# Attention and state-space heads in pairs: half-array products of two heads side by side

## The chip, the cores and the metric

One NeuronCore of one Trainium2 chip runs the whole network. The metric is the device time of one execution in microseconds (us); the time of a kernel is the median of its runs.

## The reference

The input is one sequence of 256 tokens with 1024 features, in float32. A first stack has a multi-head latent attention layer (MLA, 16 heads) with a dense SwiGLU, then a Mamba-2 layer (32 heads of 64 channels) with a mixture of eight experts. A second stack of two layers follows; each is a SwiGLU, a mixer and another SwiGLU. The mixer is what most of the change is about:

```python
h = _rms(x, mix_norm[l])
# native sparse attention (NSA), 8 heads of 64, 2 key/value groups: three softmaxes per head
o_a = gate_cmp * o_cmp + gate_sel * o_sel + gate_win * o_win
# block attention (MoBA), 8 heads of 64: with 256 tokens it is one causal softmax per head
y_a, y_b = o_a @ w_branch_nsa[l], o_b @ w_branch_moba[l]
x = x + (sigmoid(gate_a) * y_a + sigmoid(gate_b) * y_b) @ w_out[l]
```

At 256 tokens the window branch and the selected branch are both plain causal attention over all tokens, and the compressed branch has 15 keys (a block of 32 tokens every 16).

## The kernel before

Activations lie feature-major, [128 features, 256 tokens] per tile. A large product (`gemm`, `mm3`, lines 180 to 182) splits its weights into two float32r parts on ScalarE (`whi`, L153) and VectorE (`wlo`, L156) and makes three passes over 256 columns; a tile row of 256 weight columns is six such matmuls. Products of attention are plain float32, each in two passes, so a product shows as two records (x2) in the trace.

The tiles of PSUM come from four tags: `acc` (2 banks), `s` (3 banks, scores and some products), `sm` (2 banks, transposes and small things) and `po` (1 bank, outputs of attention, four heads in one bank). A tag's buffers are given out in the order of the program. The order of instructions on each engine is set when the kernel is built: a scheduler takes what its own timeline says is ready, earlier lines of the program first, and each engine then runs its list in that order. `keep_in_program_order` puts an instruction behind the one traced before it on its engine; other instructions can still come between.

In the mixer (`mixer`, twice) the order of the program is: compressed keys and values, keys and values of NSA, gates of the branches, `heads` (queries, keys) with the small products of `compress` mixed in, then eight heads of MoBA one by one, eight heads of NSA one by one (`nsa_head`), then the products for the two mixer gates (L1543, eight `gemm`s of 48 matmuls) and the branch and output products. The gate products need nothing of the attention, so the scheduler puts them into its gaps.

A MoBA head has its scores for the first and the second tile of queries (L1514, L1515; 64 rows of the array, since a head has 64 features), two mask products in bfloat16 with the identity (L1516, L1517), `softmax` (L864 to L877: two maxima on VectorE, two exponentials with sums on ScalarE, two scalings on VectorE, three transposes on TensorE, one copy on ScalarE) and two products with the values (L1520, L1521; 64 columns of the array). Even heads use rows or columns 0 to 63, odd heads 64 to 127.

An NSA head does both tiles of queries and all three branches at once: L1573 (second tile of queries against 512 keys of both branches) and L1575 (first tile), masks L1574, L1576, L1579, compressed scores L1577 and L1578 (15 columns each), maxima L1582 to L1584, six exponentials L1590, six scalings L1596, eight transposes L1602 and L1603, and for each branch the products L1613, L1614 and L1615 (the compressed one with 15 rows of the array). Its scores take two `s` banks.

MLA's heads (L839 to L846) have 128-row scores; only their products with the values are half the array. Mamba's heads have the products L1017 and L1018 with 64 columns, from `heads` inside `mamba`.

Of the kernel before, what the change touches and what calls it, by code (L numbers as in the profile page):

```python
# [17 lines left out]
P = 128  # L18
# [14 lines left out]
def _consts():  # L33
# [11 lines left out]
    # rope of the first block: rows 64..127 hold cos (32 rows) and -sin, +sin (16 rows each)  # L45
# [19 lines left out]
    # rope of the second block, feature-major, halves of 32 rows  # L65
# [8 lines left out]
    put("half2", np.stack([r < 64, r >= 64]))  # L74
    return np.concatenate(cols, 1)
# [5 lines left out]
class K:  # L81
    def __init__(self, tc, ins, out, ctx):
        self.tc, self.nc, self.i, self.out = tc, tc.nc, ins, out
        pool = lambda name, bufs, **k: ctx.enter_context(tc.tile_pool(name=name, bufs=bufs, **k))
        self.pc = pool("const", 1)
        self.pw = pool("w", 1)
        self.pn = pool("norm", 1)
        self.ps = pool("psum", 1, space=bass.MemoryType.PSUM)
        self.nraw, self.nhi, self.nlo, self.nslot = 5, 5, 4, 14
        self.fill = []  # L90
        self.fins = []
        self.lag = 0
# [5 lines left out]
        self.uid = 0  # L98

# [5 lines left out]
    # a tag's slots are given out in the order of the program: one tag for each role  # L105
# [26 lines left out]
    def parts(self, n, shape=None):  # L132
        """a pair of float32r tiles of n <= 1024 columns"""
# [9 lines left out]
    def split(self, src, pool=False):  # L143
        """[128, k, n...] float32 -> lists over k of high and low parts"""
# [16 lines left out]
    def load(self, w, k0, nk, n0, n, raw=None):  # L161
        """rows k0*128.. of w (K, N), columns n0..n0+n -> [128, nk, n]"""
# [5 lines left out]
    def wtiles(self, w, kt, n0, n, first=(), pool=False):  # L168
        """generator of (k, hi, lo): the row tiles of columns n0..n0+n, [128, n] each"""
# [7 lines left out]
    def mm3(self, out, whi, wlo, xhi, xlo, first, last):  # L177
        """out += w^T x in three float32r passes; w stationary"""
# [5 lines left out]
    def gemm(self, w, kt, n0, n, x, s=False):  # L184
        """feature-major: [n <= 256 features as 2 tiles, 256 tokens] in one bank; x = (hi, lo) [128, kt, 256]"""
# [5 lines left out]
    def gemm_steps(self, w, kt, n0, n, x, a, pool=False):  # L191
        """the same, a row tile of w at a time"""
# [8 lines left out]
    def rstd(self, *groups, bcast=True, fold=0, gap=0):  # L201
        """for each group (xs, d): [128, 256] in PSUM, (mean of squares + eps)^-1/2 of each token, on every partition"""
# [5 lines left out]
    def stats(self, *groups, fold=0):  # L208
        """halves of the means of squares + eps, token-major"""
# [21 lines left out]
    def fold(self, sqs, n):  # L231
        """adds up pairs of tiles before their products: none, those of the first pair, or all"""
# [8 lines left out]
    def sums(self, ms, sqs, first):  # L241
        """ms [128, 2]: sums over the features, token-major"""
# [7 lines left out]
    def square(self, x, part=None, new="sq"):  # L250
        """squares; added to part if there is one"""
# [7 lines left out]
    def rstd_tail(self, s, bcast=True):  # L259
        """s[:, 0]: halves of the means of squares + eps, token-major; broadcast of their ^-1/2"""  # L260
# [17 lines left out]
    def spread(self, r):  # L278
        """a token's r [128, 2] on every partition: [128, 256] in PSUM"""
# [7 lines left out]
    def norm(self, xs, d, g, hi, lo, shift=None, src=None, gap=0):  # L287
        """hi + lo = x * rstd * g (+ shift); g, shift: per-feature columns [128, len(xs)]"""
# [26 lines left out]
    def slot(self, pool, dt=F32, tag="g4", bufs=None):  # L315
        """a 4 KB tile [128, 4, 256]"""
# [10 lines left out]
    def setup(self, p):  # L327
# [12 lines left out]
        # warm the tensor engine while the first loads are under way  # L340
# [3 lines left out]
        # silu(c) as columns  # L344
# [4 lines left out]
        # the mean of the squares of each token  # L349
# [21 lines left out]
    def setup2(self):  # L371
# [17 lines left out]
        # skip weights as columns: head 2j on rows 0..63, head 2j + 1 on rows 64..127  # L389
# [8 lines left out]
    def rows(self, entries, tag, dma=None, t=None):  # L398
        """small vectors as rows of 128, transposed to columns"""
# [35 lines left out]
    def cond_mm(self, pr, rs, k0):  # L435
        """products of silu(c) with row tiles k0.., each in its own 32 columns of the array: they run at once"""
# [5 lines left out]
    def cond_sum(self, pr):  # L442
        """the sums of what cond_mm made, as columns"""
# [8 lines left out]
    def ada_steps(self, l, j, share=(), act=()):  # L452
        """closures: eight loads with their products, then the sum over partitions"""
# [40 lines left out]
    def fillers(self, jobs):  # L494
        """the steps of several jobs in a row; their sums are left to calls of fin()"""
# [51 lines left out]
        # the second mean of squares is r^2 times that of x first  # L547
# [35 lines left out]
    def resid(self, a, n0, g, last=True):  # L583
        """x += a g, for two tiles; last: what x gets last before its norm"""
# [51 lines left out]
    def rope1(self, tq, tk, p):  # L636
        """tables from the positions: rows 64.. cos, -sin, +sin; rows ..63 one"""
# [12 lines left out]
        # two pi in parts of eight bits, so that the products with n are exact  # L650
# [10 lines left out]
        # back into [-pi, pi]  # L661
# [11 lines left out]
    def mla(self):  # L673
        nc, i = self.nc, self.i
        v, mm = nc.vector, nc.tensor.matmul
        self.nslot, self.wpe = 4, 384
        with ExitStack() as c:
# [12 lines left out]
            # c_q 384 | c_kv 256 | rope 32 | rope with its halves exchanged 32  # L690
# [4 lines left out]
            def block(b):  # L695
                """the products with the two feature tiles of block b"""
# [92 lines left out]
            def latent(hl, g, xs):  # L789
                """the norm of the latents is applied to what is made of them"""  # L790
# [24 lines left out]
            # attention  # L815
            scale = float(np.float32(96.0 ** -0.5))
            um = p.tile([1, 192], BF16, name="um")
            v.memset(um[:, :64], 1.0)
            v.memset(um[:, 64:P], 0.0)
            v.memset(um[:, P:], NEG)  # L820
# [4 lines left out]
            for g in range(4):  # L825
# [7 lines left out]
                for hh in range(4):  # L833
                    if (g, hh) == (3, 0):
                        self.fin()
                    self.filler()
                    hd = g * 4 + hh
                    s = self.s([P, 384])
                    mm(s[:, :P], qT[:, hh, :P], kTa[:, hd, :P], start=True, stop=False, **kw)  # L839
                    mm(s[:, P:], qT[:, hh, P:], kTa[:, hd], start=False, stop=False, **kw)  # L840
# [3 lines left out]
                    o = po[(hh % 2) * 64 : (hh % 2) * 64 + 64, hh // 2]  # L844
                    mm(o, vs[:, 0, hd], pt[:, :T], start=True, stop=False, **kw)
                    mm(o[:, P:], vs[:, 1, hd], pt[:, T:], start=False, stop=True, **kw)  # L846
# [9 lines left out]
    def softmax(self, p, s, segs, scale, mult=None):  # L856
        """softmax of the column ranges `segs` of the scores s, transposed in blocks of 128"""
# [3 lines left out]
        w = s.shape[1]  # L861
        st = p.tile([P, 3, n], F32, tag="st", bufs=4, name=self.name("st"))
# [13 lines left out]
        pt = p.tile([P, 512], F32, tag="pt", bufs=4, name=self.name("pt"))[:, :w]  # L876
        nc.scalar.copy(pt, ptp)  # L877
        return pt

# [1 line left out]
    def mamba(self):  # L881
# [4 lines left out]
        with ExitStack() as c:  # L886
# [6 lines left out]
            def conv(n0, out):  # L893
                """out [128, 2, 256]: silu of the causal convolution of channels n0.. of xBC"""
# [13 lines left out]
            # dt: token-major, softplus; a = -exp(a_log)  # L908
# [18 lines left out]
            # log(1 + u) = 2 atanh(u / (2 + u))  # L927
# [11 lines left out]
            # running sums of dt a within each tile of tokens: columns and rows  # L939
# [50 lines left out]
            def tokens(g):  # L990
                """x dt, token-major"""
# [703 lines left out]
```

## Time and profile before

| what | value |
|---|---|
| time, median of 3 runs | 2753.67 us (2751.53 to 2759.7) |
| span of the profiled execution | 2753.1 us |
| TensorE (PE) busy | 2643.2 us, 96% |
| VectorE (DVE) busy | 2081.9 us, 76% |
| ScalarE (ACT) busy | 1578.1 us, 57% |
| GpSimd (POOL) busy | 521.4 us, 19% |
| mean granted TensorE clock | 0.970 of full speed |

Engines work at the same time, so the shares don't add up. Matmuls overlap in TensorE's pipeline: what a matmul costs is the distance from its start to the start of the next, which a timeline shows, not its own duration.

### The profile page before, as it was taken

The page shows a single profiled execution, that of the slowest core. Times are in us where ns is not written, and L with a number is a line of the kernel's source. Part 1 is how long each engine was busy: PE and PEld are TensorE (multiplying, and loading weights), DVE is VectorE, ACT ScalarE, POOL GpSimd, SP SyncE. Part 2 cuts the span into 40 slices and gives each one's busy share as a digit, 9 for nine tenths or more (in the row PEclk, how much of TensorE's full clock was granted, in tenths as well). Part 3 has the DMA queues.
Part 4 walks back from the last instruction along what each step waited for, and adds up shares of the span by engine and source line. Part 5 has one row for each costly group of instructions (what it writes and reads, how often), then busy time and mean ns, then how long its engine had stood idle before and what let it go on. Part 6 is the DMA issues. An engine that isn't in the chain of part 4 may idle for free.

```text
span 2753.1 us, 52105 instructions
## 1 busy us (share of the span) xinstructions
PE 2643.2 (96%) x21231; PEld 2531.5 (92%) x21231; DVE 2081.9 (76%) x2837; ACT 1578.1 (57%) x2330; POOL 521.4 (19%) x257
## 2 busy tenths in 40 slices
PE   7879987998999999999999999999999999999998
PEld 5779986987899999999999999978999999979998
DVE  5878999866999999899989756655755656666654
ACT  4534433663777877677777444655544444665543
POOL 4367894713100000000000110000110110000110
PEclk8979997999999999999999999999999999999999
DMA  8647775624999999899998556514555556415552
GB/s 298 216 145 239 243 230 170 216 84 132 306 350 326 369 357 352 281 355 328 365 348 290 173 180 217 157 39 146 184 181 188 184 177 212 154 36 166 182 180 94
DMA packets 577831, 608.99 MB, mean 221 GB/s; under 512 B 21563, under 2 KB 562768, under 8 KB 577584
## 3 DMA queue, kind: packets, MB, share of 16 engines
q1 hardware_dynamic: 577222, 605.26, 66.9%
q8 instruction: 168, 2.75, 0.4%
q0 software_dynamic: 176, 0.26, 0.1%
q14 instruction: 79, 0.65, 0.1%
q10 hardware_dynamic: 186, 0.07, 0.0%
HBM read 604.50 MB, written 1.05 MB: 220 GB/s over the span
## 4 chain that ended last, share of the span: by engine, by line
PE 59%; DVE 0%; POOL 0%; issue 0%; DVEq 0%; ACT 0%; POOLq 0%
PE acc L180 9%; PE acc L181 9%; PE acc L182 9%; PE s L181 3%; PE s L182 3%; PE s L180 3%; PE acc L1243 3%; PE acc L1241 3%; PE acc L1242 3%; PE acc L1264 1%; PE acc L1263 1%; PE acc L1265 1%; PE po L1613 1%; PE s L1573 1%; PE sm L1602 0%; PE sm L1414 0%
## 5 line engine op out<-in xcount | busy, mean ns | idle before, releaser
L156 DVE TENSOR_TENSOR wlo<-raw,whi 128x1024 fp32r<-128x1024 f32 (+1 forms) x815 | 1075.8, 1330 | 285.9 <-PE acc L182 190.6
L153 ACT CAST whi<-raw 128x1024 fp32r<-128x1024 f32 (+1 forms) x825 | 842.7, 1029 | 675.4 <-PE acc L181 384.2
L180 PE MATMUL acc<-hl,whi 128*128 128x256 f32 x2336 | 669.7, 287 | 1.1 <-ACT hl L304 1.1
L181 PE MATMUL acc<-hl,whi 128*128 128x256 f32 x2336 | 664.9, 285 | 5.0 <-DVE hl L305 5.0
L182 PE MATMUL acc<-hl,wlo 128*128 128x256 f32 x2336 | 664.8, 285 | 3.1 <-DVE wlo L156 3.0
L181 PEld LDWEIGHTS acc<-hl,whi 128*128 128x128 f32 x2336 | 444.9, 191 | 6.9 <-DVE hl L305 5.9
L182 PEld LDWEIGHTS acc<-hl,wlo 128*128 128x128 f32 x2336 | 444.9, 190 | 4.9 <-DVE wlo L156 4.1
L180 PEld LDWEIGHTS acc<-hl,whi 128*128 128x128 f32 x2336 | 445.3, 191 | 3.0 <-ACT hl L304 1.4
L1242 PE MATMUL acc<-wlo,xh 128*128 128x256 f32 x1408 | 397.6, 283 | 0.0
L1243 PE MATMUL acc<-whi,xl 128*128 128x256 f32 x1408 | 394.8, 281 | 0.4 <-DVE gr L1197 0.4
L1241 PE MATMUL acc<-whi,xh 128*128 128x256 f32 x1408 | 395.0, 281 | 0.0
L156 DVE TENSOR_TENSOR wlo<-more,whi 128x1024 fp32r<-128x1024 f32 x240 | 281.0, 1188 | 19.0 <-PE acc L1242 6.4
L153 ACT CAST whi<-more 128x1024 fp32r<-128x1024 f32 x244 | 246.2, 1022 | 51.1 <-PE acc L1243 23.7
L1243 PEld LDWEIGHTS acc<-whi,xl 128*128 128x128 f32 x1408 | 264.5, 188 | 0.7 <-DVE xl L1227 0.7
L1242 PEld LDWEIGHTS acc<-wlo,xh 128*128 128x128 f32 x1408 | 264.2, 188 | 0.2 <-DVE wlo L156 0.2
L1241 PEld LDWEIGHTS acc<-whi,xh 128*128 128x128 f32 x1408 | 264.1, 188 | 0.0
L182 PE MATMUL s<-hl,wlo 128*128 128x256 f32 x880 | 249.1, 283 | 0.4 <-DVE wlo L156 0.4
L181 PE MATMUL s<-hl,whi 128*128 128x256 f32 x880 | 249.4, 283 | 0.0
L180 PE MATMUL s<-hl,whi 128*128 128x256 f32 x880 | 249.1, 283 | 0.0
L256 POOL TENSOR_TENSOR part<-part,sq 128x512 f32<-128x512 f32 x20 | 31.1, 1553 | 1103.8 <-ACT sq L253 1103.8
L1264 PE MATMUL acc<-wlo,fh 128*128 128x256 f32 x704 | 195.9, 279 | 0.2 <-DVE wlo L156 0.2
L1265 PE MATMUL acc<-whi,fl 128*128 128x256 f32 x704 | 195.8, 279 | 0.0
(514 smaller groups left out, 5165.6 us busy)
## 6 DMA issues: line engine op xcount, KB each, us to landing
raw<-in_moe_w_gate_dram SPq DMA_DIRECT2D x49, 1024.0 KB, 6.5
raw<-in_moe_w_up_dram SPq DMA_DIRECT2D x49, 1024.0 KB, 7.7
raw<-in_ffn_wg_dram SPq DMA_DIRECT2D x44, 1024.0 KB, 5.2
raw<-in_ffn_wu_dram SPq DMA_DIRECT2D x44, 1024.0 KB, 5.2
more<-in_moe_w_gate_dram SPq DMA_DIRECT2D x39, 1024.0 KB, 8.1
more<-in_moe_w_up_dram SPq DMA_DIRECT2D x39, 1024.0 KB, 7.9
raw<-in_w_in_dram SPq DMA_DIRECT2D x38, 1024.0 KB, 5.0
fr<-in_ada_w_dram SPq DMA_DIRECT2D x72, 512.0 KB, 4.1
```

The source lines that it names most:

```text
L153: i = nc.scalar.copy(hi, src[:, k0 : k0 + m])
L156: (nc.gpsimd if pool else nc.vector).tensor_sub(lo, src[:, k0 : k0 + m], hi)
L180: mm(out, whi, xhi, start=first, stop=False, skip_group_check=True)
L181: mm(out, whi, xlo, start=False, stop=False, skip_group_check=True)
L182: mm(out, wlo, xhi, start=False, stop=last, skip_group_check=True)
L256: self.nc.gpsimd.tensor_add(part, part, o)
L1241: mm(a[:, b], xh[:, k], hi, start=b == 0 and k == 0, stop=False, skip_group_check=True)
L1242: mm(a[:, b], xh[:, k], lo, start=False, stop=False, skip_group_check=True)
L1243: mm(a[:, b], xl[:, k], hi, start=False, stop=k == 7, skip_group_check=True)
L1263: mm(a, fh[k], hi, start=k == 0, stop=False, skip_group_check=True)
L1264: mm(a, fh[k], lo, start=False, stop=False, skip_group_check=True)
L1265: mm(a, fl[k], hi, start=False, stop=k == FT - 1, skip_group_check=True)
```

## The change

The change issues the half-array products of two heads alternately (`side_by_side`, the second head's first), in MLA, Mamba-2 and the mixer. The scores and masks of a pair are made together into two `s` banks. NSA's window branch and its selected branch (with the compressed one) become two calls of the common `softmax` in place of one joint routine; the compressed values get 128 rows, zero but for their own 15, so that their product is as the others. In the mixer the copy of the transposed probabilities goes to ScalarE and VectorE in turn. Mask products are merged, and MLA's masks use 128 rows in place of one. Comments are taken out as well.

```diff
+    def side_by_side(self, a, b):
+        for i, (pa, pb) in enumerate(zip(a, b)):
+            for j, (o, w, x, start, stop) in enumerate((pb, pa)):
+                m = self.nc.tensor.matmul(o, w, x, start=start, stop=stop, skip_group_check=True)
+                if i or j:
+                    self.tc.keep_in_program_order(m)
...
 # mla
-                    mm(s[:, 64:128], um[:, :P], um[:, P:], start=False, stop=True, **kw)
-                    mm(s[:, 320:384], um[:, :P], um[:, P:], start=False, stop=True, **kw)
-                    pt = self.softmax(p, s, ((0, P), (P, 384)), scale)
-                    mm(o, vs[:, 0, hd], pt[:, :T], start=True, stop=False, **kw)
-                    mm(o[:, P:], vs[:, 1, hd], pt[:, T:], start=False, stop=True, **kw)
+                        mm(s.rearrange("p (a b) -> p a b", b=64)[:, 1::4], idb, um[:, None, :].broadcast_to([P, 2, 64]),
+                           start=False, stop=True, **kw)
+                        pt = self.softmax(p, s, ((0, P), (P, 384)), scale)
+                        av.append([(o, vs[:, 0, hd], pt[:, :T], True, False), (o[:, P:], vs[:, 1, hd], pt[:, T:], False, True)])
+                    self.side_by_side(*av)
...
 # softmax
-        for j, (a, b) in enumerate(segs):
+        for j, (a, b) in enumerate(segs[:2]):
             v.tensor_reduce(st[:, 0, j : j + 1], s[:, a:b], AX.X, ALU.max)
+        if n == 4:
+            v.tensor_reduce(st[:, 0, 2:4], s[:, segs[2][0] : e].rearrange("p (a b) -> p a b", a=2), AX.X, ALU.max)
-        pe = p.tile([P, self.wpe], F32, tag="pe", bufs=3, name=self.name("pe"))[:, :w]
+        pe = p.tile([P, self.wpe], F32, tag="pe", bufs=self.npe, name=self.name("pe"))[:, :w]
+        if w > e:
+            nc.gpsimd.memset(pe[:, e:], 0.0)
...
+        if gates is not None:
+            v.tensor_scalar_max(st[:, 2], st[:, 2], TINY)
         v.reciprocal(st[:, 0], st[:, 2])
+        if gates is not None:
+            v.tensor_mul(st[:, 0], st[:, 0], gates)
...
-        nc.scalar.copy(pt, ptp)
+        self.flip = not self.flip
+        (nc.scalar.copy if self.flip or self.wpe == 384 else v.tensor_copy)(pt, ptp)
...
 # mamba, heads
-                        mm(o, xd[:, 0, 2 * j + b], m[:, :T], start=True, stop=False, skip_group_check=True)
-                        mm(o[:, P:], xd[:, 1, 2 * j + b], m[:, T:], start=False, stop=True, skip_group_check=True)
+                        av.append([(o, xd[:, 0, 2 * j + b], m[:, :T], True, False), (o[:, P:], xd[:, 1, 2 * j + b], m[:, T:], False, True)])
+                    self.side_by_side(*av)
...
 # mixer
-        self.nslot, self.wpe = 4, 800
+        self.nslot, self.wpe, self.npe = 4, 512, 4
...
+            vcb = p.tile([P, 2, 2, 64], F32, name="vcb")
+            nc.gpsimd.memset(vcb, 0.0)
...
+            def scores(q, k, cmp=None):
+                ss = [self.s([P, 414 if cmp else 384]) for _ in halves]
+                ab = []
+                for s, rr in zip(ss, halves):
+                    pr = [(s[:, :P], q[rr, :P], k[rr, :P], True, False), (s[:, P:384], q[rr, P:], k[rr], False, False)]
+                    for t in range(2) if cmp else ():
+                        pr.append((s[:, 384 + 15 * t : 399 + 15 * t], q[rr, t * P : t * P + P], cmp[rr], False, False))
+                    ab.append(pr)
+                self.side_by_side(*ab)
+                for s in ss:
+                    if cmp:
+                        mm(s[:, :P], idb, mq[:, :P], start=False, stop=True, skip_group_check=True)
+                        mm(s[:, T:], idb, mq, start=False, stop=True, skip_group_check=True)
+                    else:
+                        mm(two(s)[:, 0::2], idb, mq[:, None, :P].broadcast_to([P, 2, P]), start=False, stop=True, skip_group_check=True)
+                return ss
...
-            for hd in range(8):
+            for j in range(4):
...
+                av = []
+                for b, s in enumerate(scores(qb[:, j], kb[:, j])):
+                    pt = self.softmax(p, s, ((0, P), (P, 384)), scale)
+                    o, vh = po[halves[b], j % 2], slice(j * P + b * 64, j * P + b * 64 + 64)
+                    av.append([(o, vb[:, 0, vh], pt[:, :T], True, False), (o[:, P:], vb[:, 1, vh], pt[:, T:], False, True)])
+                self.side_by_side(*av)
...
-                self.nsa_head(p, o, qa[rr, j], kd[g][rr], vsw[:, :, :, g * 64 : g * 64 + 64], vcb[:, g], gt[:, hd],
-                              idb, mq, mcp, scale)
+                for br in (1, 0):
+                    av = []
+                    segs = ((0, P), (P, 384)) if br else ((0, P), (P, 384), (384, 399), (399, 414))
+                    ss = scores(qa[:, j], kd[g][:, br * T : br * T + T], None if br else kd[g][:, 512:527])
+                    for b, s in enumerate(ss):
+                        g0 = 0 if br else 2
+                        pt = self.softmax(p, s, segs, scale, gt[:, 2 * j + b, g0 : g0 + len(segs)])
+                        o = po[halves[b], j % 2]
+                        pr = [(o, vsw[:, 0, br, vh], pt[:, :T], br == 1, False),
+                             (o[:, P:], vsw[:, 1, br, vh], pt[:, T:384], False, False)]
+                        for t in range(0 if br else 2):
+                            pr.append((o[:, t * P : t * P + P], vcb[:, t, g], pt[:, 384:], False, t == 1))
+                        av.append(pr)
+                    self.side_by_side(*av)
```

## Rows read from the trace of the kernel before

**Rows 1.** Page, the chain of waits that ended last, shares of the span by engine.
```profile
PE 59%; DVE 0%; POOL 0%; issue 0%; DVEq 0%; ACT 0%; POOLq 0%
```

**Rows 2.** Windows: MLA heads, Mamba-2 heads, mixer attention: us, busy (xinstructions), clock, DMA.
```profile
85.00:160.00 75.00, 68.04 (x451) 53.69 (x450) 57.64 (x136) 44.39 (x108) 21.11 (x10) 0.95 0.58 197
500.00:560.00 60.00, 57.87 (x496) 55.52 (x494) 54.18 (x62) 43.50 (x72) 35.65 (x14) 1.00 0.62 201
1781.00:1900.00 119.00, 119.00 (x759) 90.28 (x759) 69.01 (x186) 71.28 (x202) 8.74 (x4) 0.97 0.18 56
```

**Rows 3.** Timeline of PE, scores of a MoBA head: start us, us, line, operation.
```profile
1782.37 0.23 PE L1516 MATMUL s<-mq,idb 128*128 128x128 bf16 x1
1782.43 0.22 PE L1517 MATMUL s<-mq,idb 128*128 128x128 bf16 x1
1782.58 0.48 PE L1514 MATMUL s<-qk,qk 64*128 64x128 f32 x2
...
1783.43 0.23 PE L1516 MATMUL s<-mq,idb 128*128 128x128 bf16 x1
```

**Rows 4.** Timeline of PE, values of one MoBA head, then of two heads.
```profile
1796.61 0.65 PE L1520 MATMUL po<-pt,qk 128*64 128x256 f32 x2
...
1797.40 0.55 PE L875 MATMUL sm<-cst,pe 128*128 128x128 f32 x3
...
1811.86 0.66 PE L1520 MATMUL po<-pt,qk 128*64 128x256 f32 x4
1812.34 0.40 PE L1521 MATMUL po<-pt,qk 128*64 128x128 f32 x4
1812.56 0.59 PE L1520 MATMUL po<-pt,qk 128*64 128x256 f32 x2
```

**Rows 5.** Timeline of PE, scores and values of an NSA head.
```profile
1814.68 0.70 PE L1575 MATMUL s<-kd,qk 64*128 64x256 f32 x2
1815.31 0.28 PE L1576 MATMUL s<-mq,idb 128*128 128x256 bf16 x1
1815.52 0.39 PE L1577 MATMUL s<-kd,qk 64*128 64x15 f32 x2
...
1816.07 0.65 PE L1520 MATMUL po<-pt,qk 128*64 128x256 f32 x2
...
1816.86 0.19 PE L1579 MATMUL s<-mcp,idb 128*128 128x30 bf16 x1
...
1818.04 0.28 PE L1574 MATMUL s<-mq,idb 128*128 128x256 bf16 x1
...
1825.69 0.65 PE L1613 MATMUL po<-pt,vsw 128*64 128x256 f32 x2
...
1828.00 0.55 PE L1602 MATMUL sm<-cst,pe 128*128 128x128 f32 x3
```

**Rows 6.** Timeline of PE, values of two Mamba-2 heads.
```profile
528.78 0.66 PE L1017 MATMUL po<-m,xd 128*64 128x256 f32 x4
```

**Rows 7.** Groups by line, 1781 to 1900 us: busy, mean ns | idle before, releaser.
```profile
L156 DVE TENSOR_TENSOR wlo<-raw,whi 128x1024 fp32r<-128x1024 f32 x17 | 20.8, 1224 | 13.0 <-PE acc L182 13.0
L1590 ACT ACTIVATE pe<-s,st 128x128 f32<-128x128 f32 (+2 forms) x48 | 17.1, 374 | 13.7 <-DVE st L1585 13.7
L1590 ACT ACTIVATION_READ_ACCUMULATOR pe<-s,st 128x1 f32 x48 | 10.0, 207 | 0.0
...
L1583 DVE TENSOR_REDUCE st<-s 128x2 f32<-128x512 f32 x8 | 5.5, 692 | 6.8 <-PE s L1574 6.8
L864 DVE TENSOR_REDUCE st<-s 128x1 f32<-128x128 f32 (+1 forms) x16 | 4.8, 352 | 2.6 <-PE s L1517 2.4
L1606 DVE COPY pt<-sm 128x384 f32<-128x384 f32 x8 | 4.5, 557 | 11.9 <-PE sm L1603 11.9
...
L1582 DVE TENSOR_REDUCE st<-s 128x2 f32<-128x256 f32 x8 | 3.4, 423 | 5.6 <-PE s L1579 5.6
...
L1585 DVE TENSOR_SCALAR st<-st 128x6 f32<-128x6 f32 x8 | 1.4, 170 | 0.2
```

More of the change, by code (lines that the diff above doesn't have):

```diff
@@ L74, in _consts @@
     put("half2", np.stack([r < 64, r >= 64]))
+    put("crow", np.stack([r < 15, (r >= 15) & (r < 30)], 1))
     return np.concatenate(cols, 1)
@@ L98, in __init__ @@
         self.uid = 0
+        self.flip = False
     def name(self, s):
@@ L816, in mla @@
             scale = float(np.float32(96.0 ** -0.5))
[L817 to L820, printed above, removed]
+            idb = p.tile([P, P], BF16, name="idb1")
+            v.tensor_copy(idb, self.ident)
+            um = p.tile([P, 64], BF16, name="um")
+            v.memset(um[:64], NEG)
+            v.memset(um[64:], 0.0)
             kw = dict(skip_group_check=True)
@@ L854, in mla, with softmax @@
             self.frx = None
-    def softmax(self, p, s, segs, scale, mult=None):
+    def softmax(self, p, s, segs, scale, gates=None):
         nc = self.nc
@@ L860, in softmax @@
         n = len(segs)
-        w = s.shape[1]
-        st = p.tile([P, 3, n], F32, tag="st", bufs=4, name=self.name("st"))
-        for j, (a, b) in enumerate(segs):
+        e = segs[-1][1]
+        w = (e + P - 1) // P * P
+        st = p.tile([P, 3, n], F32, tag=f"st{n}", bufs=4, name=self.name("st"))
+        for j, (a, b) in enumerate(segs[:2]):
             v.tensor_reduce(st[:, 0, j : j + 1], s[:, a:b], AX.X, ALU.max)
+        if n == 4:
+            v.tensor_reduce(st[:, 0, 2:4], s[:, segs[2][0] : e].rearrange("p (a b) -> p a b", a=2), AX.X, ALU.max)
         v.tensor_scalar_mul(st[:, 1], st[:, 0], -scale)
-        pe = p.tile([P, self.wpe], F32, tag="pe", bufs=3, name=self.name("pe"))[:, :w]
+        pe = p.tile([P, self.wpe], F32, tag="pe", bufs=self.npe, name=self.name("pe"))[:, :w]
+        if w > e:
+            nc.gpsimd.memset(pe[:, e:], 0.0)
         for j, (a, b) in enumerate(segs):
@@ L1372, in mixer @@
             v.tensor_copy(idb, self.ident)
-            mq = p.tile([P, 2, P], BF16, name="mq")
-            for b in range(2):
-                v.tensor_copy(mq[:, b], self.c("mqk"))
-            mcp = p.tile([P, 30], BF16, name="mcp")
-            v.tensor_copy(mcp, self.c("mcmp"))
+            mq = p.tile([P, P + 30], BF16, name="mq")
+            v.tensor_copy(mq[:, :P], self.c("mqk"))
+            v.tensor_copy(mq[:, P:], self.c("mcmp"))
             gw = self.slot(p, tag="oa", bufs=2).rearrange("p a b -> p (a b)")[:, : KT * 24].rearrange("p (k n) -> p k n", k=KT)
@@ L1391, in mixer @@
             a = self.gemm(w, KT, 536, 256, h)
-            zb = p.tile([P, 800], F32, tag="pe", bufs=3, name="zb")[:, :768].rearrange("p (a b c) -> p a b c", a=2, b=3)
+            zb = self.slot(p, tag="ob", bufs=2).rearrange("p a b -> p (a b)")[:, :768].rearrange("p (a b c) -> p a b c", a=2, b=3)
             for g in range(2):
@@ L1417, in compress @@
                     v.tensor_copy(bs, ph[:, 30:31])
-                    hd = p.tile([P, 30], F32, tag="hid", bufs=2, name=self.name("hid"))
-                    nc.scalar.activation(hd, ph[:, :30], AF.Gelu_apprx_tanh, bias=bs)
+                    hd = p.tile([P, 30 + 30 * b], F32, tag="hid" + "kv"[b], bufs=1, name=self.name("hid"))
+                    for n in range(1 + b):
+                        o = hd.rearrange("p (g n c) -> p g n c", g=2, c=15)[:, :, n]
+                        nc.scalar.activation(o, ph[:, :30].rearrange("p (g c) -> p g c", g=2), AF.Gelu_apprx_tanh, bias=bs)
                     hid.append(hd)
@@ L1430, in compress @@
                 v.tensor_mul(tc_[:, 1], pk[:, 1, :30], self.c("sinE"))
-                pv = self.sm([15, 2, 64])
+                pv = self.sm([30, 2, 64])
                 for g in range(2):
                     v.tensor_add(kd[g][:, 512:527], tc_[:, 0, g * 15 : g * 15 + 15], tc_[:, 1, g * 15 : g * 15 + 15])
-                    mm(pv[:, g], hid[1][:, g * 15 : g * 15 + 15], w2[:, 4], start=True, stop=True)
-                v.tensor_copy(vcb, pv)
+                    mm(pv[:, g], hid[1][:, g * 30 : g * 30 + 30], w2[:, 4], start=True, stop=True)
+                for t in range(2):
+                    v.tensor_scalar_mul(vcb[:30, t], pv, self.c("crow")[:30, t : t + 1])
             a = self.acc()
@@ L1505, in outs @@
                 v.tensor_sub(o[1], po, o[0])
+            halves = (slice(0, 64), slice(64, 128))
+            two = lambda a: a.rearrange("p (a b) -> p a b", b=P)
+            def scores(q, k, cmp=None):
[14 more added lines that the diff above has]
+                return ss
@@ L1523, in mixer @@
                     outs(po, ob, j - 1)
             oa = [self.slot(p, F32R, "oa", 2) for _ in range(2)]
-            for hd in range(8):
-                if hd % 4 == 0:
+            for j in range(4):
+                if j % 2 == 0:
                     po = self.po()
-                rr, j, g = slice((hd % 2) * 64, (hd % 2) * 64 + 64), hd // 2, hd // 4
-                o = po[rr, j % 2]
-                self.nsa_head(p, o, qa[rr, j], kd[g][rr], vsw[:, :, :, g * 64 : g * 64 + 64], vcb[:, g], gt[:, hd],
-                              idb, mq, mcp, scale)
-                if hd % 4 == 3:
+                g = j // 2
+                vh = slice(g * 64, g * 64 + 64)
+                for br in (1, 0):
+                    av = []
+                    segs = ((0, P), (P, 384)) if br else ((0, P), (P, 384), (384, 399), (399, 414))
[10 more added lines that the diff above has]
+                    self.side_by_side(*av)
+                if j % 2:
```

95 lines of the change are left out of this document (18 added, 77 removed).

## The prediction

> **What bounds the kernel now.** I read the chain of waits first. It is followed back from the end and runs, as far as it reaches, on TensorE alone: 59% of the span, and 0% on every other engine [rows 1]. It reaches back to the experts' middle and so covers both mixers; for MLA and Mamba-2 it says nothing. So I took windows of the changed stages next. In the first mixer's attention (1781 to 1900 us) TensorE is busy for all of 119.0 us, VectorE for 69.0 and ScalarE for 71.3 [rows 2]. The list of waits of that stretch has no wait of TensorE. The groups by line say the same from the other side: VectorE waits for scores (6.8 and 5.6 us), for transposes (11.9) and for the gate products to free its buffers (13.0), each time for TensorE [rows 7]. Every microsecond that TensorE need not spend there can come back, as long as gate products fill its gaps. The second mixer repeats the pattern and I count it like the first. MLA is different: TensorE is busy for 68.0 of 75 us, the other engines less, and latency shows. In Mamba-2 TensorE has 57.9 of 60 us and VectorE 54.2 [rows 2]. Last I read the timeline of TensorE in these windows, from start to start.
>
> **What runs side by side already.** One row decides much. Two MoBA heads whose value products happen to be adjacent (four records, x4) take from 1811.86 to 1812.34, 0.48 us, for their 256 columns, and 0.22 for the 128 that follow [rows 4]. A head alone takes 0.79 us in all (1796.61 to 1797.40), the change of shape at its end included. So two products on different 64-column halves cost one. Mamba-2's pairs look the same, and 13 of its 16 are adjacent already; one row stands for them [rows 6]. For 64-row halves, the scores, no row shows two heads adjacent, since masks of the full array stand between. The nearest row is the column pair. Bounds: nothing saved, or one product for two. I take the second, because here too each half has its own inputs and the outputs go to two banks; both stay in the range.
>
> The Trainium skill, page "TensorE: Matmul & The Clock Gate", section "Measured speedup vs the span model", gives 3.07 times for four row tiles where 4 would be full, a rate that no run here shows. If two tiles kept that share of the ideal, a pair would cost 1.3 heads, an estimate by that page, and about 4 us a layer would be missing from the sum below.
>
> **The change, part by part.** A full-array mask block of 128 columns takes 0.06 us (1782.37 to 1782.43), and going to the half-array shape costs 0.15 - 0.06 = 0.09 [rows 3].
>
> MoBA scores, eight heads a layer: one head takes 1.06 us, 0.85 of it scores (1782.58 to 1783.43) [rows 3]. A pair will take 0.09 + 0.85 + 4 x 0.06 = 1.18 in place of 2.12. Four pairs save 3.8 us.
>
> MoBA values: 0.79 + 0.09 = 0.88 each time. The layer has seven such times now (six heads alone, one pair) and will have four: 2.7 us saved.
>
> NSA, per head now: scores and masks 1814.68 to 1816.07 and 1816.86 to 1818.04 (between them stands another head's product), two mask blocks behind that, one change of shape: 1.39 + 1.18 + 0.12 + 0.09 = 2.78. Values 1825.69 to 1828.00: 2.31 + 0.09 = 2.40 [rows 5]. Two heads: 10.4. After, per pair: window scores as MoBA's, 1.18. Selected scores 0.09 + 0.85, the compressed ones 0.55 (1815.52 to 1816.07 [rows 5]), five mask blocks 0.30: 1.79. Window values 0.88; selected values 0.88, and two compressed products on 128 rows at 0.22 each [rows 4]: 1.32. Sum 5.2. Saved 5.2 a pair, 20.8 a layer. Two transposes in sixteen go as well; they count for nothing here.
>
> A layer: 3.8 + 2.7 + 20.8 = 27.3 us of TensorE, two layers 54.6.
>
> What it adds. VectorE, per NSA head: four maxima of 0.352 for 0.692 + 0.423, and four small operations (scale, floor, reciprocal, gate) once more at 0.17 [rows 7]: 0.97, or 7.8 us a layer. Every second copy of a MoBA head moves to VectorE: 4 x 0.557 = 2.2. Half of NSA's copies grow from 384 to 512 columns: 0.7 by their columns. So 69.0 becomes 79.7 us. ScalarE loses four MoBA copies and all 15-row copies; its other copies grow a little. POOL gets eight memsets of 98 columns a layer, which only the transposes wait for; no row prices them, and POOL is busy for 8.7 of 119 us [rows 2], so I count nothing; if they came late, the exponentials and scalings of the same tile, several us, would cover them.
>
> The stretch then needs 119.0 - 27.3 = 91.7 us of TensorE against 79.7 of VectorE, 87%. The nearest row is Mamba-2: VectorE at 90% while TensorE is busy for 96% [rows 2]. New waits work against that. A pair takes two of the three score banks, so the next pair's first scores (its second head, issued first) wait for an exponential; and no value product starts before both heads' copies are made. Behind such a wait on TensorE's queue stand transposes and gate products in the planned order. I take 95%: 91.7 / 0.95 = 96.5 us, 22.5 saved a layer, 45 in all.
>
> The Trainium skill, page "TensorEngine Tiling (Array Packing)", sections "PSUM Bottleneck" and "Gotcha 1: PSUM Pressure", speaks against more: tiling speeds up the products and not the emptying of PSUM, and row tiles need banks of their own. The rows above agree so far that VectorE's share rises from 58% to 87%; that it becomes the bound is the third case below.
>
> MLA: at most 8 x 0.88 = 7.0 us of values, and for the one-row masks up to one change of shape a head, 16 x 0.09 = 1.4 [rows 3, 4], 8.4 in all. But TensorE idles there for 7 of 75 us, and VectorE has 57.6 [rows 2]. Between 0 and 8 I take 3.
>
> Mamba-2: three pairs that are not adjacent yet, 3 x 0.88 = 2.6 at most; against it the first head waits for the second, so it could lose as much. I take 1.
>
> Sum: 45 + 3 + 1 = 49 us off a span of 2753.1, 2704; the median of the runs lies 0.6 above that span, so 2705.
>
> **The rivals.** A: as above. Own range: all TensorE time comes back (55 + 8 + 3), and the stretch at the lower clock goes, which costs 0.03 x 119 = 3.6 us now (granted clock 0.97 [rows 2], part of it at 1.2 in place of 2.4 GHz): 2684. At 88% in place of 95% the stretch takes 104 us, 15 saved a layer: 2723. Chance 0.60.
>
> B: row halves don't overlap. Lost are 0.85 of each MoBA pair and 0.85 + 0.85 + 0.55 of each NSA pair, 12.4 a layer, so 14.9 remain. For it: no row. Against it: the column pair [rows 4]. VectorE is then at 77% and TensorE stays full: 2753.7 - 30 - 3 = 2721. Chance 0.10.
>
> C: softmax becomes the bound. For it: 87% of VectorE and two of three banks held. If TensorE is busy for only 83%, the stretch takes 110 us, 9 saved a layer: 2753.7 - 18 - 1 = 2735, at the worst 2749. Against it: today VectorE waits for TensorE and not the other way [rows 7]. Chance 0.16.
>
> D: slower. The mixer has twelve pair steps a layer (four MoBA, eight NSA). With 119 us there, it is slower as soon as a step takes over 9.9 us on average. One pair at a time, nothing overlapped: scores, first maxima, both heads' exponentials at 0.374 + 0.207 a piece on ScalarE, second head's scalings, transposes, copy and values. For the selected branch that is 1.8 + 1.1 + 4.6 + 1.9 + 0.4 + 0.7 + 1.3 = 11.8 us, where scalings and transposes are estimates from maxima and score products of like width; a window or MoBA step is about 7.2. Four times 26.2 is 105. With the gate products' splits in between (20.8 [rows 7]) it is 125, 6 more a layer, so 2753.7 + 12 - 2 = 2764. Against it: the third bank and four buffers of probabilities let steps overlap. Chance 0.07.
>
> E: the change doesn't do what it says: planned products come between the two halves, the shape changes as often as now, and only merged masks are left, some 4 us: 2750. Against it: a pair's products become ready together. Chance 0.07.
>
> **How the numbers follow.** What can be told from no change is 0.3%, 8.3 us. Faster: A, B and most of C, 0.84. Same: the rest of C and most of E, 0.08. Slower: D and a little of E, 0.08. The range 2684 to 2744 leaves out the low end of A (0.03), the worst of C (0.02), E and D: 0.19.
>
> **What would show it.** Value and score products of two heads as rows of x4 within 0.02 us of each other, a score pair taking 0.85 us: A, not B. The mixer's attention ending some 22 us sooner with TensorE still near 95% busy: A. Waits of TensorE for exponentials or scalings of several us in total: C, and over 9.9 us a step: D. The prediction is wrong if TensorE starves once its products are cheap, if more time at the lower clock follows from such gaps, or if MLA moves by more than 8 us.

## The result and the profile after

The changed kernel takes 2713.82 us (median of 4 runs, 2709.8 to 2720.05) beside 2756.68 for the kernel before on the same chip (2751.53 to 2759.99): a ratio of 0.9846, 95% interval 0.9824 to 0.9867. The forecast was 2705 in a range of 2684 to 2744, faster with a chance of 0.84. The time is in the range and in the likeliest case's own range; the gain is 43 us where I counted 49.

The head of the page of the profile after, and its chain of waits:

```profile
span 2707.9 us, 52231 instructions
...
PE 2593.0 (96%) x21247; PEld 2516.0 (93%) x21247; DVE 2088.0 (77%) x2943; ACT 1573.2 (58%) x2296; POOL 523.9 (19%) x275
...
PE 58%; DVE 0%; POOL 0%; issue 0%; ACT 0%; DVEq 0%; POOLq 0%
```

The chain still runs on TensorE alone, as in [rows 1]; TensorE is 50 us less busy, VectorE 6 us more. Windows of MLA's heads, of Mamba-2's stage from the dense FFN's end to its own, and of the first mixer's attention, columns as in [rows 2]:

```profile
85.00:160.00 75.00, 63.22 (x458) 54.78 (x458) 59.57 (x138) 45.92 (x109) 25.47 (x12) 0.91 0.60 199
405.40:677.00 271.60, 234.47 (x1810) 220.69 (x1810) 213.26 (x340) 142.36 (x253) 124.59 (x57) 0.89 0.47 151
1775.00:1881.00 106.00, 105.16 (x838) 88.93 (x838) 78.13 (x239) 71.74 (x187) 11.13 (x12) 1.00 0.26 82
```

The window of the mixer's attention is 106 us long, where that of [rows 2] is 119. It holds as many gate products (385 records of them, 388 before) and also 63 records of the products of MoBA's branch, which stood behind the window before. TensorE is busy for 99% of it and VectorE for 78.1 us, 74% (I had counted 79.7). What VectorE waits for there (us in all, times, longest):

```profile
DVE st L892 <- ACT pe L889: 4.4, 4, 2.4
DVE wlo L159 <- ACT oa L1535: 4.3, 1, 4.3
DVE st L881 <- PE s L1556: 3.8, 2, 3.0
DVE pt L903 <- PE sm L900: 2.9, 5, 0.8
```

In [rows 7] it waited 13.0 us for gate products and 11.9 for transposes; it waits less for TensorE now, but TensorE's only wait in this window is 0.7 us long. So TensorE is still the bound, and time that it need not spend there should still come back.

**Where the time went.** I cut each execution at the last update of the residual that ends a stage. A mixer is then the stretch from the end of the FFN before it to its own end, branch and output products included:

| kernel | time, us | first mixer | second mixer |
|---|---|---|---|
| before | 2756.7 | 237.2 | 233.9 |
| changed | 2713.8 | 216.0 | 216.0 |

Before, a stretch of 6.8 us at 1.2 GHz (granted clock 0.50) lies in the first mixer, though TensorE was busy for all of the 44 us before it:

```profile
1844.40:1851.20 6.80, 6.80 (x27) 5.17 (x27) 2.57 (x8) 3.79 (x16) 0.00 (x0) 0.50 0.01 2
```

Counted at half its length, 3.4 us, it leaves 233.8 for that mixer, as long as the other, and the change is worth 17.9 us in each. The two mixers together give 39.1 of the 45.2 us by which the spans of the two profiled executions differ (2753.1 and 2707.9). Summed from start to start over the second mixer, TensorE spends 18.3 us on scores in place of 24.9, 13.6 on values in place of 23.9, 1.5 less on transposes, 0.4 less on masks and 0.8 more on all else: nearly the whole gain lies in the half-array products.

**The pairs in the trace.** TensorE's timeline at the start of the first attention (start, duration, line, operation; all half-array products have line L320 now, gate products L183 to L185):

```profile
1774.96 0.70 PE L320 MATMUL s<-qk,qk 64*128 64x256 f32 x4
1775.60 0.39 PE L1556 MATMUL s<-mq,idb 128*128 128x256 bf16 x2
1775.92 0.49 PE L320 MATMUL s<-qk,qk 64*128 64x128 f32 x2
1776.33 0.39 PE L183 MATMUL acc<-hl,whi 128*128 128x256 f32 x1
1776.55 0.29 PE L184 MATMUL acc<-hl,whi 128*128 128x256 f32 x1
...
1781.63 0.92 PE L320 MATMUL s<-qk,qk 64*128 64x128 f32 x6
1782.48 0.39 PE L1556 MATMUL s<-mq,idb 128*128 128x256 bf16 x2
...
1789.13 0.65 PE L320 MATMUL po<-pt,qk 128*64 128x256 f32 x2
1789.70 0.70 PE L320 MATMUL s<-qk,qk 64*128 64x256 f32 x2
1790.33 0.86 PE L320 MATMUL po<-pt,qk 128*64 128x256 f32 x6
...
1797.17 0.87 PE L320 MATMUL po<-pt,qk 128*64 128x256 f32 x8
1797.97 0.92 PE L320 MATMUL s<-qk,qk 64*128 64x128 f32 x6
```

A float32 product leaves two records, so a whole pair with two products a head (MoBA's or the window's) is x8, and a pair of the selected branch, with four a head, x16. Two heads' values take 0.80 us (1797.17 to 1797.97), what one head took in [rows 4]; and the x4 at 1774.96, both heads' 256 score columns, takes 0.64, where one head's took 0.63 (1814.68 to 1815.31 in [rows 5]). Column halves and row halves both overlap. But many pairs are broken. The second head's first score product is issued alone at 1775.92, costs 0.41 us and then 0.10 for the change of shape back (1776.33 to 1776.55 where 0.12 is usual); 5.3 us later the other three follow and take the same 0.85 that a whole pair would. At 1789.13 the same happens to a value product, 0.57 us. In the second mixer eleven of the twelve score steps have such a lone product, and four value steps. A selected pair of values that stayed whole takes 1.24 us:

```profile
2436.75 0.87 PE L320 MATMUL po<-pt,vsw 128*64 128x256 f32 x8
2437.45 0.61 PE L320 MATMUL po<-pt,vcb 128*64 128x128 f32 x8
2437.99 0.55 PE L900 MATMUL sm<-cst,pe 128*128 128x128 f32 x3
```

### The profile page after: what moved, and what is told of

It reads as the page before. It is cut to its first block, busy times and chain, and to the rows that moved or that the text cites. A ratio compares the mean times of both kernels' runs of the same rounds, so it can differ in the third digit from the quotient of the medians.

```text
span 2707.9 us, 52231 instructions
## 1 busy us (share of the span) xinstructions
PE 2593.0 (96%) x21247; PEld 2516.0 (93%) x21247; DVE 2088.0 (77%) x2943; ACT 1573.2 (58%) x2296; POOL 523.9 (19%) x275
## 4 chain that ended last, share of the span: by engine, by line
PE 58%; DVE 0%; POOL 0%; issue 0%; ACT 0%; DVEq 0%; POOLq 0%
PE acc L183 9%; PE acc L184 9%; PE acc L185 9%; PE s L185 3%; PE s L184 3%; PE s L183 3%; PE acc L1269 3%; PE acc L1270 3%; PE acc L1271 3%; PE acc L1292 1%; PE acc L1291 1%; PE acc L1293 1%; PE s L320 1%; PE po L320 1%; PE sm L900 1%; PE sm L1441 0%
## 5 line engine op out<-in xcount | busy, mean ns | idle before, releaser
L183 PE MATMUL acc<-hl,whi 128*128 128x256 f32 x2336 | 668.3, 286 | 1.6 <-ACT hl L307 1.1
L185 PE MATMUL acc<-hl,wlo 128*128 128x256 f32 x2336 | 662.8, 284 | 4.4 <-DVE wlo L159 4.4
L185 PEld LDWEIGHTS acc<-hl,wlo 128*128 128x128 f32 x2336 | 444.1, 190 | 5.3 <-DVE wlo L159 4.8
L183 PEld LDWEIGHTS acc<-hl,whi 128*128 128x128 f32 x2336 | 444.2, 190 | 4.2 <-ACT hl L307 1.4
L185 PE MATMUL s<-hl,wlo 128*128 128x256 f32 x880 | 248.7, 283 | 0.2 <-DVE wlo L159 0.2
L183 PE MATMUL s<-hl,whi 128*128 128x256 f32 x880 | 248.5, 282 | 0.0
```

The costliest lines, as they stand in the source:

```text
L183: mm(out, whi, xhi, start=first, stop=False, skip_group_check=True)
L185: mm(out, wlo, xhi, start=False, stop=last, skip_group_check=True)
```

## The experiments

Each changes the two mixers of the changed kernel unless it says otherwise. The ratio is to the kernel before on the same chip.

| run | time, us | ratio, 95% interval | mixers, us |
|---|---|---|---|
| scores and values head by head | 2727.97 | 0.9913, 0.9892 to 0.9933 | 222.5, 222.5 |
| scores head by head | 2722.83 | 0.9887, 0.9866 to 0.9908 | 219.6, 219.5 |
| masks first | 2705.18 | 0.9828, 0.9798 to 0.9858 | 212.9, 211.3 |
| MLA and Mamba-2 as before | 2719.56 | 0.9880, 0.9863 to 0.9897 | 216.0, 216.0 |
| values apart | 2732.91 | 0.9920, 0.9895 to 0.9944 | 223.9, 225.4 |
| scores and values apart | 2742.64 | 0.9966, 0.9948 to 0.9985 | 229.9, 229.9 |
| masks first, window last | 2711.09 | 0.9841, 0.9821 to 0.9861 | 215.3, 215.1 |
| masks first, head by head | 2721.66 | 0.9884, 0.9841 to 0.9927 | 217.3, 217.3 |
| changed, again | 2714.16 | 0.9844, 0.9831 to 0.9858 | 216.1, 216.0 |
| masks first, again | 2707.76 | 0.9829, 0.9816 to 0.9842 | 211.4, 211.3 |

A mixer's length repeats within 0.1 us where no stretch at 1.2 GHz lies in it (there is one of 3.4 us, costing 1.7, in the 212.9, the 225.4, the 215.3 and the 215.1), so it tells more than the time, which moves by 10 us between runs of one kernel.

**Both products head by head** (all of the second head's, then all of the first's).

```diff
-                self.side_by_side(*ab)
+                self.one_by_one(*ab)
...
-                self.side_by_side(*av)
+                self.one_by_one(*av)
...
+    def one_by_one(self, a, b):
+        for i, (o, w, x, start, stop) in enumerate(list(b) + list(a)):
...
```

> The changed kernel, but in the two mixers a pair's products are issued head by head (all of the second head, then all of the first) in place of alternately; pairs, merged masks, softmax and planning stay. Theory (the products that run side by side make the gain): a score pair loses 0.57 to 0.85 us and a value pair 0.48 to 0.70 in the eight window and MoBA steps of a layer, 2.0 to 2.5 in the four selected steps, 16 to 22 a layer less some 6 that broken pairs lose already; TensorE is 99% busy there, so it comes back in full: 2735 to 2747 us. Rival (fewer changes of shape, merged masks and the evened softmax make the gain): within 6 us of the changed kernel's 2714.

It came out between the two, 14 us slower. The timeline shows why: a pair of window values, a selected pair of values, and what follows it.

```profile
1822.65 0.88 PE L326 MATMUL po<-pt,vsw 128*64 128x256 f32 x8
1823.46 0.39 PE L184 MATMUL acc<-hl,whi 128*128 128x256 f32 x1
...
1835.10 0.87 PE L326 MATMUL po<-pt,vsw 128*64 128x256 f32 x4
1835.81 0.27 PE L326 MATMUL po<-pt,vcb 128*64 128x128 f32 x1
1835.81 0.43 PE L326 MATMUL po<-pt,vsw 128*64 128x256 f32 x1
...
1837.04 0.55 PE L906 MATMUL sm<-cst,pe 128*128 128x128 f32 x3
```

The window pair still takes 0.8 us for its eight records, although all of one head's products now stand before the other's: its four 256-column records come before its four 128-column ones, so the heads ran at once. In the selected pair the first head has eight records; the other starts when the fifth of these does, 0.71 us in, and the pair takes 1.94 us. So the edit had not taken the value pairs apart, only the selected ones in part; of the scores, the planning put the masks of one head between the two heads, and each head's window scores stand alone.

**Scores head by head** (only the call with `*ab`):

> The changed kernel, but only the score products (64-row halves) of the mixers' pairs are issued head by head; value products stay alternate. Theory (row halves run side by side as column halves do): 9 to 12 us a layer less some 4 that broken pairs lose already, 10 to 17 in all: 2724 to 2731 us. Rival (row halves give nothing, all the gain comes from values and masks): 2714, within 4.

3.5 us a mixer and 9.0 in all, where 10 to 17 were expected: row halves do run side by side, and taking them apart costs less than counted. Summed from start to start over the second mixer, the scores take 24.6 us in place of 18.3, 6.3 more, as counted for a layer (9 to 12 less 4); values, masks and the large products take 3.9 less and transposes 1.3 more. One head's selected scores, alone here, take 1.20 us:

```profile
2408.57 1.27 PE L326 MATMUL s<-kd,qk 64*128 64x128 f32 x8
2409.77 0.23 PE L1559 MATMUL s<-mq,idb 128*128 128x128 bf16 x1
```

The order of the value products costs the other 3.0 of the run above, close to the 4 x 0.7 that its selected pairs lose (1.94 against 1.24).

**Masks first.** Each head's masks start its bank, the scores are added to them, and the first score product is tied behind both masks.

```diff
-                if i or j:
+                if i or j or pin:
...
+                for s in ss:
...
+                        m = mm(two(s)[:, 0::2], idb, mq[:, None, :P].broadcast_to([P, 2, P]), start=True, stop=False, skip_group_check=True)
...
-                self.side_by_side(*ab)
+                self.side_by_side(*ab, pin=True)
```

> The changed kernel, but in the mixers' score steps the mask products come first and the score products are added to them, so that both heads' banks are taken before the first score product is issued. Theory (what is missing from the forecast of the mixers is lost where the first product of a pair is issued alone, 0.49 us and a change of shape each, at nine of twelve score steps and four of twelve value steps of a layer): most pairs stay whole, 4 to 6 us a layer come back, 2702 to 2706 us, and TensorE's rows show few lone products. Rival (the gaps were filled anyway, or holding two banks earlier makes the next steps wait): 2712 or more.

A mixer takes 211.3, 4.7 us less. Its timeline, a window pair and a selected pair with the rows next to them, then TensorE's wait from 2366 to 2470 us:

```profile
2375.65 0.28 PE L1549 MATMUL s<-mq,idb 128*128 128x256 bf16 x1
2375.86 0.93 PE L320 MATMUL s<-qk,qk 64*128 64x128 f32 x8
2376.72 0.28 PE L1549 MATMUL s<-mq,idb 128*128 128x256 bf16 x1
...
2443.54 1.28 PE L320 MATMUL s<-kd,qk 64*128 64x128 f32 x16
2444.75 0.33 PE L900 MATMUL sm<-cst,pe 128*128 128x128 f32 x1
```

```profile
PE sm L900 <- DVE pe L897: 2.1, 2, 1.3
```

A whole pair (x8) takes 0.86 us, where one head took 0.85 in [rows 3], and a whole selected one (x16) 1.21, where one head alone took 1.20: one head's time for two. All value pairs are whole now too, though the edit didn't touch them. The expectation counted nine broken score steps from the planned order; the trace has eleven. At 0.51 each, and four value steps at 0.57, that is 7.9 us a mixer. What doesn't come back is the wait above, 2.1 us, and steps that are still broken: three of the twelve begin with a lone product, and in others transposes stand between the two heads. The edit moves the masks and ties the first product at once; no run tells which of the two made the pairs whole.

**MLA and Mamba-2 as before** (their loops taken from the kernel before):

> The changed kernel with MLA's attention and Mamba-2's products as before; only the mixers are changed. Theory (Mamba-2's pairing itself makes its stage 3 to 5 us shorter, MLA's is given back in the dense FFN): Mamba-2's stage is back at 275 to 277 us, time 2717 to 2719, and the dense FFN ends at the same place. Rival (Mamba-2's stage became shorter through the clock alone): stage and time stay within 2 us of the changed kernel's, 2714, wherever the stretches at half clock are as long.

The time is about what the theory says, its mechanism is not. Mamba-2's stage in the kernel before, in this run, and in the one with masks first, which has the pairs:

```profile
405.50:682.40 276.90, 238.24 (x1810) 221.10 (x1810) 217.56 (x340) 141.70 (x253) 124.31 (x57) 0.88 0.46 149
```

```profile
407.80:676.90 269.10, 233.52 (x1810) 218.34 (x1810) 217.71 (x341) 141.76 (x253) 123.37 (x57) 0.89 0.48 154
```

```profile
401.00:680.90 279.90, 238.88 (x1810) 224.03 (x1810) 215.20 (x340) 142.24 (x253) 124.61 (x57) 0.86 0.46 147
```

The second, without the pairs, is the shortest of all twelve executions, the third, with them, the longest; the granted clock (0.89 and 0.86) goes along with that, the pairs don't (276.9 at 0.88 without them in the kernel before). Mamba-2's pairing is worth nothing that can be seen. MLA's change can be seen: MLA ends at 175.5 and 179.2 us in the two executions with its old loop, and at 171.0 to 173.9 in the ten with the new one. The dense FFN behind MLA ends at 405.5 and 407.8 us in the two executions with the old MLA, at 397.5 to 406.3 (mean 402.3) in the ten with the new one.

**Values apart** (each head's value products issued right behind its softmax):

```diff
...
-                self.side_by_side(*av)
+                    mm(o, vb[:, 0, vh], pt[:, :T], start=True, stop=False, skip_group_check=True)
+                    mm(o[:, P:], vb[:, 1, vh], pt[:, T:], start=False, stop=True, skip_group_check=True)
...
```

> The changed kernel, but in the mixers each head's value products are issued right behind its own softmax, free for the planning, in place of in pairs; scores stay in pairs. Theory (two heads' column halves run side by side wherever they stand adjacent; a head alone costs what a pair costs, 0.80 us and a change of shape, 1.23 in the selected branch): six of the eight window and MoBA pairs of a layer fall apart and lose 0.9 us each, the four selected pairs 1.3 each; the four broken value steps of the changed kernel no longer cost extra, 2.7: a mixer goes from 216.0 to about 224 us, the kernel from 2714 to some 2730. Rival (value pairs give next to nothing): a mixer within 2 us of 216.

223.9 us as counted. In its timeline a pair that fell together by chance, and a head alone:

```profile
2396.74 0.66 PE L1568 MATMUL po<-pt,qk 128*64 128x256 f32 x4
2397.22 0.40 PE L1569 MATMUL po<-pt,qk 128*64 128x128 f32 x4
...
2404.00 0.65 PE L1568 MATMUL po<-pt,qk 128*64 128x256 f32 x2
2404.48 0.38 PE L1569 MATMUL po<-pt,qk 128*64 128x128 f32 x2
```

Both take 0.48 us for the 256 columns.

**Scores and values apart** (this and the edit of the scores together):

> The changed kernel with both kinds of pairs apart in the mixers: scores head by head, each head's value products right behind its softmax. Merged masks, the split of a head's branches, the common softmax and the spread of the copies stay. Theory (most of the mixers' gain is products side by side): about 8 us more a layer than the kernel with one head's products after the other's (222.5 us a mixer), 230, against 233.9 before: some 2742 us. Rival (half of the gain or more is the rest of the change): a mixer at 226 or less, 2734 us or less.

229.9: with no pair intended (two value pairs of the second mixer fell together all the same), 4.0 of the 17.9 us remain for merged masks, the split of the branches and the common softmax; 13.9 are the pairs as they are, 18.6 the pairs with masks first.

**Masks first, window last** (`for br in (0, 1)`, with the start flag moved):

> The kernel with masks first (2705 us, 211.3 us a mixer), but of each pair's two NSA branches the selected one comes first and the window, with the shorter softmax, last. Theory (TensorE's 2 us of idle time at the end of attention, where it waits for the scalings of the last selected pair, come from that pair's long chain): 1 to 2 us a mixer, 2702 us. Rival (the chain ends elsewhere, or the selected scores now come where the banks are short): 211 or more, 2705 or more.

The rival: 215.1, or 213.4 without its stretch at 1.2 GHz. TensorE's waits of the second attention, and the place:

```profile
PE s L1549 <- ACT pe L889: 3.1, 1, 3.1
PE po L320 <- DVE pt L903: 0.4, 1, 0.4
```

```profile
2459.20 0.35 PE L1549 MATMUL s<-mq,idb 128*128 128x256 bf16 x1 [3.11 <-ACT pe L889]
```

The wait for scalings is gone, but the last window pair's mask now waits 3.1 us for a score bank that the selected pair's exponentials still hold.

**Masks first, head by head** (`one_by_one` in the kernel with masks first):

> The kernel with masks first, but inside a pair all products of the second head come before those of the first, as before in the run with one head after the other; here the two heads stay adjacent. Theory (TensorE starts a product on the other half while products of the first half are still queued, up to four records ahead, as the value pairs of that run show: eight records in 0.81 us): window and MoBA pairs cost the same as alternately, selected pairs 0.7 us more for values and as much for scores, 5 to 6 us a layer: 216 to 217 us a mixer, 2715 us. Rival A (row halves overlap only when issued alternately): 0.85 us more for each whole score pair, 220 or more. Rival B (the order inside a pair never matters): 211 to 212.

217.3, near the theory. A whole window score pair, with the row behind it:

```profile
2378.98 0.93 PE L326 MATMUL s<-qk,qk 64*128 64x128 f32 x8
2379.84 0.28 PE L1555 MATMUL s<-mq,idb 128*128 128x256 bf16 x1
```

0.86 us, as alternately. Row halves don't need the alternate order either, as long as nothing stands between the heads and a head has no more than two products. With four products it matters: a whole selected pair takes 1.96 us for its scores and 1.94 for its values, in place of 1.21 and 1.24, and the mixer takes 6.0 us more than with the heads alternating, more than the 4.7 that masks first gained. The time of the kernel scatters here from 2707 to 2729 us and says little. A selected score pair, with the row behind it:

```profile
2449.64 2.03 PE L326 MATMUL s<-kd,qk 64*128 64x128 f32 x16
2451.60 0.33 PE L906 MATMUL sm<-cst,pe 128*128 128x128 f32 x1
```

**Changed kernel and masks first, side by side.**

> The changed kernel itself once more, beside the next one on the same chip. Both theories: 2714 us, within 4; a mixer takes 216.0 us.

> The kernel with masks first once more, beside the changed kernel on the same chip. Theory (whole pairs are worth 4.7 us a mixer and nothing else differs): 211.3 us a mixer, 9 us less than the changed kernel in all, about 2705 us. Rival (the difference of the first runs was the scatter of MLA and Mamba-2): within 3 us of the changed kernel.

The mixers repeat (216.0 and 211.3). In time masks first is 6.4 us ahead in the medians, of 9.4 expected; the two intervals still touch, so as a whole-kernel gain it is likely and not settled. It has the lowest median of all kernels here.

## Why the prediction was right, and where it was off

**TensorE's sum.** Right in mechanism. Two heads cost one: values 0.80 us, scores 0.86 with masks first (I took 0.85), selected values 1.24 (counted: 1.32), selected scores 1.21 (counted: 0.85 and 0.55). Transposes, counted at nothing, gave 1.5 a mixer. Rival B is out by those rows and by the run with scores head by head. The 27.3 us a layer stand for whole pairs, filled to 95%, 22.5. With masks first a mixer saves 22.6.

**What was mis-sized.** The term of 22.5 us saved a layer measured 17.9 in the changed kernel. The step that failed is the sentence against rival E, that "a pair's products become ready together". They don't: the second head's first product is planned as soon as one bank (or, for values, one copy) is ready, for only the products behind it are tied to their place. I had charged new waits to TensorE as idle time, 5%; in fact it is busy for 99%, and the loss sits in lone half-array products and changes of shape, work that a busy share can't show. Masks first gave 4.7 of it back, as much as was missing. That this meets the 22.5 so closely is partly luck: the 5% stood for idle time, of which 2.1 us are there, and the rest of the 4.7 us that this falls short of 27.3 is mostly steps still broken.

**Luck in the total.** The time came nearer to the forecast than its main term. The mixers' products gave 35.7 us where I counted 45. In the profiled pair 3.4 us of lower clock and the 5.3 us by which Mamba-2's stage was shorter fell the same way; neither is shown to be the change's.

**Softmax (C), slower (D), nothing (E).** VectorE came to 78.1 us, but 74% of the longer stretch, and TensorE hardly waits: no C, no D. E happened in part, as said. The Trainium skill, page "TensorEngine Tiling (Array Packing)", section "PSUM Bottleneck", says that after a fourfold speedup by tiling the emptying of PSUM may become the bound. With two heads side by side it did not: TensorE waits for 0.7 of 106 us. The Trainium skill, page "TensorE: Matmul & The Clock Gate", section "Measured speedup vs the span model", has 3.07 times for four row tiles. Two tiles lost less here and ran 1.98 times as fast as one (2 x 0.85 / 0.86).

**MLA and Mamba-2.** MLA, counted at 3 us, does end sooner: by 2.8 us in the profiled pair, and all ten ends with the new loop lie before both with the old one. How much of it the whole keeps is not shown: the FFN behind it ends where it did in the profiled pair, and 4 us sooner in the mean, with a scatter of 9 between executions. Mamba-2, counted at 1, shows 0; of its sixteen pairs fourteen stood together before, not thirteen, so there was even less to gain. The 5.3 us by which its stage was shorter in the profiled pair aren't the pairing's; some 3.4 of them, an estimate by half their length, are stretches at 1.2 GHz (68 us of them before, 61 after). The rest, and the longer stretch of the experts and the SwiGLU behind them in the run with MLA and Mamba-2 as before (1029.7 against 1022.9 us, where 34 us in place of 24 lie at 1.2 GHz), stay open.

**The clock.** The 3.6 us of the lower clock, which I had put into the low end of my range alone, did go in the first mixer: it has no such stretch after, and 3.4 us came back there beside the sum. Whether the change removed it is not shown: the kernel before has one profiled execution, and three of the ten runs above have a stretch of 3.4 us in a mixer.

## What to carry to other kernels

In these runs the half-array products of two heads cost one, for float32 and for both kinds of halves, but only while nothing stands between them: look in the timeline for x2 where x4 or x8 should be, because a busy TensorE hides it. Tie the first product of a pair too, behind something that needs both heads' banks (here both masks). Alternate the heads within the pair: with two products a head the order made no difference, with four it cost 0.7 us a pair. A stage whose length repeats to 0.1 us tells edits apart that the kernel's time can't.

## What the runs showed of the hardware that was not expected

Products of the two column halves don't wait for each other's place in TensorE's queue: issued head by head, the second head started 0.01 us behind the first while that one's other records were still to come, and 0.71 us behind it where the first had eight records, with its fifth. The Trainium skill, page "TensorE: Matmul & The Clock Gate", section "The mechanism", says that matmuls start and end strictly in order. By that rule the head-by-head pair would take some 1.4 us, an estimate (0.6 until the first head's last record starts, 0.8 for the second head); it took 0.81, and the measurement decides. Row halves did the same: 0.86 us for the eight records of a score pair issued head by head.

Mamba-2's stage ran from 269.1 to 279.9 us over twelve profiled executions, with 58 to 78 us of it at 1.2 GHz, whatever its products' order: a difference of a few microseconds there means nothing in a single profile.
